# Level products of a gated recurrence in 32-column parts of TensorE, and pair products in its row halves

## The chip, the cores and the metric

The kernel runs on one core of one Trainium2 chip. The metric is the device time of one execution in microseconds (us). TensorE is called PE below, its weight loads PEld, VectorE DVE, ScalarE ACT, GpSimd POOL. A line number such as L1396 is the line of the kernel that issued an instruction.

## The reference, cut to what matters

One decoder layer: RMSNorm, one wide projection `w_in` of the normed rows (256 prompt tokens and 8 sequences of 8 sampled tokens, 320 rows in all), two recurrent branches, two projections merged by gates, an output projection and a final norm. Both recurrences are evaluated in blocks of tokens.

Branch A (16 heads of 64 channels, RWKV-7) is a delta rule with a matrix state:

```
s = s * w_t - (s kk_t)(kk_t * a_t)^T + v_t k_t^T ;  y_t = s r_t
```

Branch B (8 heads of 128 channels, HGRN2) is a gated linear recurrence:

```
b = cumsum(log_g);  o = (q * exp(b)) @ s
att[t, s] = sum_d q[t, d] k[s, d] exp(b[t, d] - b[s, d])   for s <= t, else 0
o += att @ v;       s = exp(b_last) * s + (k * exp(b_last - b))^T v
```

The change touches how `att` of branch B, and the matrix of all pairs of tokens in a block of 64 (`g2`) of branch A, are computed.

## The kernel before, in words

After a start stage that norms and transposes the inputs, one long stage computes the projection and both recurrences, head pair by head pair (`p` from 0 to 7: two heads of branch A, one of branch B). Its streams are the matmuls of the big projection (tile `mps`): weights are split into two float32r parts, `whi` and `wlo`, and each weight tile of 128x128 meets the 320 rows three times. All other matmuls of this stage (tiles `a`, `b`, `y`, called small products here) belong to the recurrences. They are plain float32, and each stands in the trace as two passes, two pairs of a weight load and a matmul.

The order of this stage is made by `Recorder`: every operation is recorded (so nearly all carry line L1396), `link` finds what depends on what, and `order` runs a list schedule over the engines with modelled costs. On PE a small product that is ready goes ahead of the streams. A product whose weights have at most 64 rows or columns uses a part of the array and has a `mode` other than (128, 128); such products wait until at least `APART` = 10 streams have run since the last of their kind, and those of `hgrn` until they have been ready for `WAIT` = 6000 ns (as the model sees it), so that several can share one change of the array's mode. After the eighth head pair the gate tiles of `NFILL` = 4 further column blocks (`sga`) are streams that the last head's recurrence can run beside. Then the merging stage begins (L338 to L340, with its own main tiles first, then `ppa` and `ppb`), and last the output stage (`po`).

In `rwkv`, `bk2` holds for each of four blocks of 64 prompt tokens (and a fifth block of 64 sampled tokens) the decayed keys, with two heads of 64 channels stacked on the partitions. `arp` holds the queries with zeros for the other head, so that one product of 128 rows gives both heads' pairs: five products of 128x128 weights with 256 columns, in three PSUM tiles `pg`. DVE multiplies them by the mask `mk` into `g2`.

In `hgrn`, `level(sz, tag)` makes the decayed keys and queries (`kq`) for pairs of neighbouring blocks of `sz` tokens with ACT (exponentials) and DVE (products), and moves the running decays `F` and `R` up one level. `products` multiplies 128 tokens by 128 tokens, twice (`j` = 0, 1), although only blocks on the diagonal are kept; `keep` copies those by the mask `mu8` into `att`, which POOL clears first for each head. The order is: products inside blocks of 8 (`k0`, `q0`) and of level 8; the states' products `pos` of the eight sampled sequences (`qz` by `s0`, 32 columns of weights each, in four column parts of the array); the work on the sampled states; levels 16, 32 and 64 with their products (`pl`); then the products with `vt`.

Of the kernel before, what the change touches and what calls it, by code (L numbers as in the profile page):

```python
# [9 lines left out]
F32 = mybir.dt.float32  # L10
# [7 lines left out]
NP_ = 256  # L18
# [29 lines left out]

class Op:
    __slots__ = ("eng", "fn", "args", "kw", "cost", "lat", "uses", "mode", "passes", "cols", "stream",  # L50
                 "succ", "npred", "ready", "rank", "block", "margin", "wait", "port", "hold", "dma", "n")


def span_of(ap):
# [14 lines left out]
class Recorder:  # L69
# [2 lines left out]

    def __init__(self, engines, is_big):
        self.real, self.ops, self.spans, self.is_big = engines, [], {}, is_big
        self.block, self.wait = None, 0

    def proxy(self, eng):
        rec, real = self, self.real[eng]
# [6 lines left out]
    def add(self, eng, name, fn, args, kw):  # L85
# [16 lines left out]
        o.lat = self.LAT[eng]  # L102
        o.dma = "dma" in name
        o.mode = None
        o.block = self.block
# [5 lines left out]
        if eng == "PE":  # L111
# [41 lines left out]

    def link(self):

        writers, readers = {}, {}
        for o in self.ops:
            o.succ, pred = [], {}
            for name, p0, p1, m, wr, psum in o.uses:
# [22 lines left out]
            o.npred = len(pred)  # L182
            for q, data in pred.values():
# [90 lines left out]
def hybrid_step(ctx, tc, x_prompt, x_sample, state_rwkv, state_hgrn, state_shift, norm_g, w_in,  # L274
# [19 lines left out]
    def ctile(shape, name, dt=F32, pool=rconst):  # L294
        return pool.tile(shape, dt, name=name, tag=name)
# [59 lines left out]
    with tc.tile_pool(name="start", bufs=1) as st, \  # L355
# [59 lines left out]
        def keep_ge(ap, pattern, base, cm, fill=0.0):  # L415
            G.affine_select(out=ap, in_=ap, pattern=pattern, compare_op=ALU.is_ge, fill=fill,
                            base=base, channel_multiplier=cm)
# [36 lines left out]
                         mk[:, 0, x].rearrange("p (s i) -> p s i", i=8), blk)  # L454


        mf = st.tile([64, 3, 64], F32, name="mf")
        mu8 = ctile([128, 3, 64], "mu8", U8)
        G.memset(mf, 1.0)
        for n, sz in enumerate((8, 8, 16)):  # L460
            if n == 0:
                mfh = mf[:, 0].rearrange("p (b i) -> p b i", i=8)
                keep_ge(mf[:, 0], [[1, 64]], 0, -1)
                keep_ge(mfh, [[-8, 8], [0, 8]], 0, 1)
                keep_ge(mfh, [[8, 8], [0, 8]], 7, -1)
                continue
            lv = mf[:, n].rearrange("p (b two s) -> p b two s", two=2, s=sz)
            nb = 32 // sz
# [216 lines left out]
    def ring(pool, tag, shape, bufs, dt, size, clear=False):  # L685
# [12 lines left out]
        if len(shape) == 2:  # L698
# [2 lines left out]
        return t_.rearrange(f"p ({' '.join(names)}) -> p {' '.join(names)}", **dict(zip(names, shape[1:])))  # L701

    SIZES = {"uK": 384, "uS": 384, "uE": 384, "uA": 320, "uB": 384, "uQ": 320, "big": 512, "s0t": 512, "v": 384,
             "w1": 384, "w2": 320, "w3": 320, "ks": 128, "ket": 256}


    CLEAR = {"uB", "uE", "ys", "rhs", "rhs2", "k3", "vm", "w1", "vt"}

    def at(name, shape=(128, NT), tag=None, bufs=1, dt=F32):
        tag = tag or name  # L710
# [48 lines left out]
    def rwkv(p, r, k, vp, za):  # L759
# [105 lines left out]

        g2 = at("g2", (128, 5, 2, 2, 64))
        M = at("M", (128, 3, 2, 64), tag="uE")
        for g in range(3):
            ps = aps("pg")
            n = 2 if g < 2 else 1  # L870
            for c_ in range(n):
                ci = 2 * g + c_
                T.matmul(ps[:, 256 * c_:256 * c_ + 256], bk2[:, ci].rearrange("p j t -> p (j t)"),
                         arp[:, ci].rearrange("p x h t -> p (x h t)"), start=True, stop=True)
            m = mk[:, 0:2] if g < 2 else mk[:, 2:3]
            V.tensor_mul(g2[:, 2 * g:2 * g + n].rearrange("p c x h t -> p (c x) h t"),
                         ps[:, :256 * n].rearrange("p (a h t) -> p a h t", h=2, t=64),
                         m.rearrange("p c x t -> p (c x) t")[:, :, None].to_broadcast([128, 2 * n, 2, 64]))


        half = lambda ps, n: ps[:, :192 * n].rearrange("p (a x t) -> p a x t", a=n, x=3)[:, :, 0:3:2]
# [243 lines left out]
    def hgrn(hd, q, k, v, zb):  # L1125
# [40 lines left out]
        V.tensor_mul(k0[:, :NT], k0[:, :NT], k)  # L1166

        att = bt("att", (128, 2 * 128 + 64))
        G.memset(att, 0.0)

        def level(sz, tag):
            half = lambda t_: t_[:, :NP_].rearrange("p (b two s) -> p b two s", two=2, s=sz)
            kq = bt("kq", (128, NP_), tag=tag)
            if sz in (32, 64):

                side = [kq[:, 128 * x:128 * x + 128].rearrange("p (b s) -> p b s", s=sz) for x in range(2)]
            else:
                side = [half(kq)[:, :, x] for x in range(2)]
            for x, e in enumerate((R, F)):
                S.activation(side[x], half(e)[:, :, x], AF.Exp)  # L1180
# [10 lines left out]
        def products(ps, o_, kq, q_):  # L1191
            for j in range(2):
                tk_ = slice(128 * j, 128 * j + 128)
                T.matmul(ps[:, o_ + 128 * j:o_ + 128 * j + 128], kq[:, tk_], q_[:, tk_], start=True, stop=True)

        def keep(ps, o_, n):
            own = lambda t_, c_: t_.rearrange("p (j c t) -> p j c t", c=2, t=64)[:, :, c_]
            for c_ in range(2):
                sl = HS[c_]
                V.copy_predicated(own(att[sl, :NP_], c_), mu8[sl, None, n].to_broadcast([64, 2, 64]),  # L1200
                                  own(ps[sl, o_:o_ + NP_], c_))
# [16 lines left out]
        V.tensor_mul(es[:, 1], es[:, 1], k[:, NP_:])  # L1218

        ps = bps("pos")  # L1220
        for si in range(NSEQ):
            j = si % 4
            T.matmul(ps[32 * j:32 * j + 32, 128 * (si // 4):128 * (si // 4) + 128], qz[:, si, :], s0[:, si, :],
                     start=True, stop=True)
# [37 lines left out]
        for j in range(2):  # L1262
            for b in range(2):
                o_ = 64 * j + 32 * b
                V.tensor_copy(att[64 * b:64 * b + 32, 128 * j + 64 * b + 32:128 * j + 64 * b + 64],
                              ps[o_:o_ + 32, 256 + o_:288 + o_])
            V.tensor_copy(att[0:64, 128 * j + 64:128 * j + 128], ps[HS[j], 384 + 64 * j:448 + 64 * j])

        kq128 = bt("kq", (128, 2, 128), tag="w3")
        ke = bt("ke", (128, 128), tag="w1")  # L1270
# [40 lines left out]
    def shift_state():  # L1311
        for g, (s_, n) in enumerate(((0, 5), (5, 4))):
# [265 lines left out]
```

## Time and profile before

| | before |
|---|---|
| median of 3 runs | 1157.26 us (1156.6 to 1157.67) |
| the profiled execution's own time | 1155.96 us |
| its span, first to last instruction | 1154.3 us |
| mean granted clock of PE | 0.998 |
| busy share of the span: PE, DVE, ACT, POOL | 98%, 67%, 58%, 18% |

A row of the trace that begins with two numbers gives start and length in us. A group gives a count, then the busy time and the mean length of one. PE's matmuls overlap: one that is listed with 0.31 us may be followed by the next after 0.15 us, so the distance between starts is what a matmul costs, not its length.

### The profile page before, as it was taken

To read this page: it belongs to the slowest core of one execution; us is meant where nothing else is said; L and a number is where in the kernel's file an instruction comes from. 1 tells how busy PE (TensorE), PEld (TensorE's weight loads), DVE (VectorE), ACT (ScalarE), POOL (GpSimd) and SP (SyncE) were. 2 spreads that over 40 slices of the span, in tenths; PEclk is the share of its full clock that TensorE was granted. 3 is DMA by queue.
4 is the path that set the end of the run, shared out by engine and by line. 5 is a ranking of instruction groups with operands and counts; after the bars stand their busy time and mean duration, and the time that the engine had idled before them with its cause. 6 is when DMAs were issued, how large, how long until landed. Compare 5 with 4: busy or idle time off the path is not lost.

```text
span 1154.3 us, 20774 instructions
## 1 busy us (share of the span) xinstructions
PE 1135.7 (98%) x7816; PEld 1097.9 (95%) x7816; DVE 775.9 (67%) x1634; ACT 669.2 (58%) x1483; POOL 208.0 (18%) x405
## 2 busy tenths in 40 slices
PE   6999999999999999999999999999999999999997
PEld 6999999999999999999999999999999999998886
DVE  8778878877887888878788686544444444436632
ACT  6766766667666667567667667444444444435322
POOL 9432223222311321421321310000000000000000
PEclk9999999999999999999999999999999999999999
DMA  6745435535445435436435434555555555577512
GB/s 180 199 117 127 129 102 136 142 92 132 129 113 146 117 93 150 131 81 169 120 93 162 115 105 132 148 152 153 152 147 148 151 154 151 146 253 254 182 41 91
DMA packets 283096, 159.69 MB, mean 138 GB/s; under 512 B 22893, under 2 KB 273264, under 8 KB 282356
## 3 DMA queue, kind: packets, MB, share of 16 engines
q1 hardware_dynamic: 282996, 158.37, 48.6%
q8 instruction: 61, 1.00, 0.4%
q14 instruction: 39, 0.32, 0.1%
HBM read 148.53 MB, written 9.81 MB: 137 GB/s over the span
## 4 chain that ended last, share of the span: by engine, by line
PE 96%; POOL 2%; DVE 1%; ACT 1%; issue 0%; DMA 0%; ACTq 0%; POOLq 0%
PE mps L1396 41%; PE a L1396 13%; PE mps L338 6%; PE mps L340 6%; PE mps L339 6%; PE b L1396 4%; PE po L1479 3%; PE po L1481 3%; PE po L1480 3%; PE ppb L338 2%; PE ppa L338 2%; PE ppb L340 2%; PE ppa L340 2%; PE ppa L339 2%; PE ppb L339 2%; PE po L1484 1%
## 5 line engine op out<-in xcount | busy, mean ns | idle before, releaser
L1396 PE MATMUL mps<-hhi,wlo 128*128 128x320 f32 x1088 | 344.9, 317 | 0.0
L1396 PE MATMUL mps<-hlo,whi 128*128 128x320 f32 x1088 | 344.7, 317 | 0.0
L1396 PE MATMUL mps<-hhi,whi 128*128 128x320 f32 x1088 | 344.6, 317 | 0.0
L1396 PEld LDWEIGHTS mps<-hlo,whi 128*128 128x128 f32 x1088 | 204.9, 188 | 3.3 <-issue 3.0
L1396 PEld LDWEIGHTS mps<-hhi,wlo 128*128 128x128 f32 x1088 | 205.0, 188 | 2.7 <-issue 2.4
L1396 PEld LDWEIGHTS mps<-hhi,whi 128*128 128x128 f32 x1088 | 205.0, 188 | 0.8 <-issue 0.4
L329 DVE TENSOR_TENSOR wlo<-raw,whi 128x1024 fp32r<-128x1024 f32 x88 | 107.8, 1225 | 125.0 <-ACT whi L328 124.8
L328 ACT CAST whi<-raw 128x1024 fp32r<-128x1024 f32 x88 | 92.3, 1048 | 163.3 <-PE mps L339 104.8
L1396 ACT CAST whi<-raw 128x1024 fp32r<-128x1024 f32 x134 | 140.6, 1049 | 77.2 <-PE mps L1396 75.8
L1396 DVE TENSOR_TENSOR wlo<-raw,whi 128x1024 fp32r<-128x1024 f32 x134 | 167.5, 1250 | 24.4 <-ACT whi L1396 23.1
L339 PE MATMUL mps<-hlo,whi 128*128 128x320 f32 x448 | 138.5, 309 | 0.0
L338 PE MATMUL mps<-hhi,whi 128*128 128x320 f32 x448 | 138.5, 309 | 0.0
L340 PE MATMUL mps<-hhi,wlo 128*128 128x320 f32 x448 | 138.5, 309 | 0.0
L340 PEld LDWEIGHTS mps<-hhi,wlo 128*128 128x128 f32 x448 | 84.1, 188 | 0.0
L338 PEld LDWEIGHTS mps<-hhi,whi 128*128 128x128 f32 x448 | 84.1, 188 | 0.0
L339 PEld LDWEIGHTS mps<-hlo,whi 128*128 128x128 f32 x448 | 84.1, 188 | 0.0
L1468 DVE TENSOR_TENSOR wlo<-raw,whi 128x1024 fp32r<-128x1024 f32 x32 | 38.5, 1222 | 39.1 <-ACT whi L1467 39.0
L1467 ACT CAST whi<-raw 128x1024 fp32r<-128x1024 f32 x32 | 33.1, 1051 | 48.4 <-DMA raw<-in_w_out_dram 22.4
L1479 PE MATMUL po<-whi,mhi 128*128 128x512 f32 x128 | 50.1, 391 | 0.7 <-DVE gbt L1436 0.7
L1481 PE MATMUL po<-wlo,mhi 128*128 128x512 f32 x128 | 50.0, 391 | 0.0
L1480 PE MATMUL po<-whi,mlo 128*128 128x512 f32 x128 | 50.0, 391 | 0.0
L339 PE MATMUL ppb<-ybl,whi 128*128 128x320 f32 x128 | 39.6, 309 | 0.0
(409 smaller groups left out, 2304.0 us busy)
## 6 DMA issues: line engine op xcount, KB each, us to landing
raw<-in_w_in_dram SPq DMA_DIRECT2D x194, 512.0 KB
raw<-in_w_out_dram SPq DMA_DIRECT2D x32, 512.0 KB
raw<-in_proj_a_dram SPq DMA_DIRECT2D x16, 512.0 KB
raw<-in_proj_b_dram SPq DMA_DIRECT2D x16, 512.0 KB
s<-in_state_hgrn_dram SPq DMA_DIRECT2D x8, 512.0 KB
out_dram<-s SPq DMA_DIRECT2D x8, 512.0 KB
s<-in_state_rwkv_dram SPq DMA_DIRECT2D x8, 256.0 KB
out_dram<-s SPq DMA_DIRECT2D x8, 256.0 KB
```

The costliest lines, as they stand in the source:

```text
L328: S.copy(hi[:, ks], raw[:, ks])
L329: sub.tensor_sub(lo[:, ks], raw[:, ks], hi[:, ks].bitcast(F32))
L338: T.matmul(dst, hi[:, q, :], xhi[:, k, :], start=(k == 0), stop=False)
L339: T.matmul(dst, hi[:, q, :], xlo[:, k, :], start=False, stop=False)
L340: T.matmul(dst, lo[:, q, :], xhi[:, k, :], start=False, stop=(k == nk - 1))
L1396: o.fn(*o.args, **o.kw)
L1467: S.copy(hi, raw)
L1468: V.tensor_sub(lo, raw, hi.bitcast(F32))
L1479: T.matmul(pt, h, hi, start=first, stop=False)
L1480: T.matmul(pt, l, hi, start=False, stop=False)
L1481: T.matmul(pt, h, lo, start=False, stop=end)
L1484: T.matmul(pt, h, hi, start=first, stop=False)
```

## The change

In `rwkv` the pair products of the four prompt blocks become eight: for each head 64 rows (`HS[h]`) of `bk2` and `arp`, 128 columns of weights and 128 columns that stream, the two heads alternating in the upper and lower row half of the array, each head in a PSUM tile of its own. The fifth product stays. DVE's masking multiplications stay three, with other views.

In `hgrn` all four levels are made at once, before the states' products. Every level product is now made by 32 tokens: 32 columns of weights and 32 that stream (64 at the last level), in the column part where those 32 tokens lie, so that the result holds only tokens of one block of 32. There are 34 of them, recorded right behind the eight states' products in one group: 24 for the first three levels, 4 for level 32, 4 for level 64, 2 for the sampled tokens. They replace nine products of full weight tiles. Masks shrink to 32x32; three masked copies of DVE go to a new tile `attc`, four copies of ACT move its blocks to `att`, two masked copies take the sampled tokens, and the six copies of levels 32 and 64 stay. `att` and `attc` are cleared once. `kq16`, `kq32` and `kq64` use other buffers.

`Recorder` gets groups: the members of one share their dependencies and the highest rank of them, so that they stand together on PE, and a cost that counts all parts of the array as running at once.

```diff
@@ Recorder.add
-            o.cost = o.passes * max(load, stream / min(2, 128 // o.mode[1]))
+            side = 128 // o.mode[1] * (128 // o.mode[0] if o.group else 1)
+            o.cost = o.passes * max(max(load, stream) / side, 7) if o.group else o.passes * max(load, stream / min(2, side))
@@ Recorder.link
+        for members in groups.values():
+            own = {o.n for o in members}
+            shared = {}
+            for o in members:
+                for n, (q, data) in preds[o.n].items():
+                    if n not in own:
+                        shared[n] = q, data or shared.get(n, (q, False))[1]
+            for o in members:
+                preds[o.n].update(shared)
...
+        for members in groups.values():
+            top = max(o.rank for o in members)
+            for o in members:
+                o.rank = top
@@ start stage
-        mf = st.tile([64, 3, 64], F32, name="mf")
-        mu8 = ctile([128, 3, 64], "mu8", U8)
+        mf = st.tile([32, 3, 32], F32, name="mf")
+        mu8 = ctile([128, 3, 32], "mu8", U8)
...
-        for sl in HS:
-            G.tensor_copy(mu8[sl], mf)
+        for g in range(4):
+            G.tensor_copy(mu8[32 * g:32 * g + 32], mf)
@@ rwkv
-        for g in range(3):
-            ps = aps("pg")
-            n = 2 if g < 2 else 1
-            for c_ in range(n):
-                ci = 2 * g + c_
-                T.matmul(ps[:, 256 * c_:256 * c_ + 256], bk2[:, ci].rearrange("p j t -> p (j t)"),
-                         arp[:, ci].rearrange("p x h t -> p (x h t)"), start=True, stop=True)
...
+        banks = [aps("pg") for _ in HS]
+        side_by_side([((banks[h][:, 128 * ci:128 * ci + 128], bk2[HS[h], ci].rearrange("p j t -> p (j t)"),
+                        arp[HS[h], ci, :, h]), dict(start=True, stop=True)) for ci in range(4) for h in range(2)])
+        for h in range(2):
+            V.tensor_mul(g2[:, 0:4, :, h].rearrange("p (a c) x t -> p a (c x) t", c=2),
+                         banks[h].rearrange("p (a c t) -> p a c t", a=2, t=64),
+                         mk[:, 0:2].rearrange("p c x t -> p (c x) t")[:, None].to_broadcast([128, 2, 4, 64]))
+        ps = aps("pg")
+        T.matmul(ps[:, :256], bk2[:, 4].rearrange("p j t -> p (j t)"), arp[:, 4].rearrange("p x h t -> p (x h t)"),
+                 start=True, stop=True)
@@ hgrn
         att = bt("att", (128, 2 * 128 + 64))
-        G.memset(att, 0.0)
...
-        kq8 = level(8, "w2")
-        ps = bps("pg")
-        products(ps, 0, k0, q0)
-        products(ps, 256, kq8, kq8)
-        keep(ps, 0, 0)
-        keep(ps, 256, 1)
+        kq8, kq16, kq32, kq64 = level(8, "w2"), level(16, "o"), level(32, "ket"), level(64, ("s1", "ks"))
...
+        work = [((ps[32 * j:32 * j + 32, 128 * g:128 * g + 128], qz[:, 4 * g + j], s0[:, 4 * g + j]))
+                for g in range(2) for j in range(4)]
+        tile32 = lambda g, c0, a_, b_: work.append((pg[32 * g:32 * g + 32, c0:c0 + b_.shape[-1]], a_, b_))
+        for n, (a_, b_) in enumerate(((k0, q0), (kq8, kq8), (kq16, kq16))):
+            for j in range(2):
+                for g in range(4):
+                    tk_ = slice(128 * j + 32 * g, 128 * j + 32 * g + 32)
+                    tile32(g, 64 * n + 32 * j, a_[:, tk_], b_[:, tk_])
+        for g in range(4):
+            tile32(g, 192, kq32[0][:, 32 * g:32 * g + 32], kq32[1][:, 32 * g:32 * g + 32])
+        for g in range(4):
+            tile32(g, 224, kq64[0][:, 32 * g:32 * g + 32], kq64[1][:, 64 * (g // 2):64 * (g // 2) + 64])
+        for g in range(2):
+            tk_ = slice(NP_ + 32 * g, NP_ + 32 * g + 32)
+            tile32(g, 288, k0[:, tk_], q0[:, tk_])
+        side_by_side([(x_, dict(start=True, stop=True)) for x_ in work])
+        attc = bt("attc", (128, 2, 32))
+        for n in range(3):
+            V.copy_predicated(attc, mu8[:, None, n].to_broadcast([128, 2, 32]),
+                              pg[:, 64 * n:64 * n + 64].rearrange("p (j t) -> p j t", t=32))
+        for g in range(4):
+            own = slice(32 * g, 32 * g + 32)
+            S.copy(att[own, :NP_].rearrange("p (j t) -> p j t", j=2)[:, :, own], attc[own])
+            if g < 2:
+                V.copy_predicated(att[own, NP_ + 32 * g:NP_ + 32 * g + 32], mu8[own, 0], pg[own, 288:320])
...
-        T.matmul(ps[:, 128:192], k0[:, NP_:], q0[:, NP_:], start=True, stop=True)
-        V.copy_predicated(att[0:64, NP_:], mu8[0:64, 0], ps[0:64, 128:192])
...
-        kq16, kq32, kq64 = level(16, "w3"), level(32, "w2"), level(64, "w1")
-        ps = bps("pl")
-        products(ps, 0, kq16, kq16)
-        T.matmul(ps[:, 256:384], kq32[:, 0:128], kq32[:, 128:256], start=True, stop=True)
-        T.matmul(ps[:, 384:512], kq64[:, 0:128], kq64[:, 128:256], start=True, stop=True)
-        keep(ps, 0, 2)
@@ new
+    def side_by_side(products):
+        book.group = len(book.ops)
+        for args, kw in products:
+            T.matmul(*args, **kw)
+        book.group = None
```

## Rows read from the trace of the kernel before

**Rows 1.** The page: span, busy time of each engine, chain by engine.
```profile
span 1154.3 us, 20774 instructions
PE 1135.7 (98%) x7816; PEld 1097.9 (95%) x7816; DVE 775.9 (67%) x1634; ACT 669.2 (58%) x1483; POOL 208.0 (18%) x405
PE 96%; POOL 2%; DVE 1%; ACT 1%; issue 0%; DMA 0%; ACTq 0%; POOLq 0%
```
**Rows 2.** Busy time by engine, recurrence stage: length, PE, PEld, DVE, ACT, POOL, granted clock.
```profile
30.00:700.00 670.00, 668.98 (x4905) 653.58 (x4904) 543.60 (x1333) 451.39 (x1146) 179.83 (x349) 1.00 0.46 126
```
**Rows 3.** PE's waits: total us, times, longest.
```profile
PE mps L591 <- POOL wlo L598: 0.6, 1, 0.6
```
**Rows 4.** Timeline of PE around one head pair's pair products (`arp`, `bk`).
```profile
62.69 0.31 PE L1396 MATMUL mps<-hhi,wlo 128*128 128x320 f32 x1
62.84 2.32 PE L1396 MATMUL a<-arp,bk 128*128 128x256 f32 x10
64.81 0.50 PE L1396 MATMUL mps<-hhi,whi 128*128 128x320 f32 x1
65.14 0.31 PE L1396 MATMUL mps<-hlo,whi 128*128 128x320 f32 x1
```
**Rows 5.** Instructions on tiles `w`: durations min/median/max, first and last start, forms.
```profile
L1396 PE MATMUL b<-w x96: 270/275/377, 91.2 to 681.2; 128*128 128x128 f32 x96
L1396 PE MATMUL b<-w,w x48: 217/275/275, 90.1 to 669.7; 128*128 128x128 f32 x32, 128*128 128x64 f32 x16
```
**Rows 6.** Timeline of PE at two runs of level products, a stream between.
```profile
666.58 0.61 PE L1396 MATMUL b<-w,w 128*128 128x128 f32 x4
666.94 0.39 PE L1396 MATMUL mps<-hhi,wlo 128*128 128x320 f32 x1
667.17 0.60 PE L1396 MATMUL b<-w 128*128 128x128 f32 x4
```
**Rows 7.** Timeline of PE around the states' products of the last head.
```profile
676.05 0.31 PE L1396 MATMUL mps<-hhi,whi 128*128 128x320 f32 x1
676.29 0.64 PE L1396 MATMUL b<-s,qz 128*32 128x128 f32 x16
676.86 0.41 PE L1396 MATMUL mps<-hlo,whi 128*128 128x320 f32 x1
677.11 0.27 PE L1396 MATMUL a<-ident,sr 128*128 128x128 f32 x1
```
**Rows 8.** The first head's states' products, matmuls begun by 100.772 and by 101.3.
```profile
100.75 0.32 PE L1396 MATMUL b<-s,qz 128*32 128x128 f32 x4
...
100.75 0.64 PE L1396 MATMUL b<-s,qz 128*32 128x128 f32 x16
```
**Rows 9.** Their weight loads begun by 100.88, when four matmuls had begun.
```profile
100.75 0.16 PEld L1396 LDWEIGHTS b<-s,qz 128*32 128x32 f32 x8 [0.19 <-issue]
```
**Rows 10.** Instructions on tile `att`.
```profile
L1396 DVE COPY_PREDICATED att<-mu,b x56: 214/296/313, 92.0 to 683.2; 64x128 f32<-64x128 uint8 x48, 64x64 f32<-64x64 uint8 x8
L1396 POOL MEMSET att<- x8: 358/364/373, 39.5 to 619.8; 128x320 f32 x8
```
**Rows 11.** Groups by shape: the nearest ACT copy, and POOL's mask work.
```profile
L1396 ACT COPY uE<-uB 64x64 f32<-64x64 f32 x16 | 3.9, 245 | 0.2
...
L473 POOL CAST mu<-mf 64x192 uint8<-64x192 f32 x2 | 2.2, 1098 | 0.1
...
L416 POOL TENSOR_SCALAR_AFFINE_SELECT mf<-mf 64x64 f32<-64x64 f32 x3 | 1.2, 416 | 0.0
```
**Rows 12.** Instructions on tile `arp`: the pair products of all heads.
```profile
L1396 PE MATMUL a<-arp,bk x80: 377/379/380, 62.8 to 640.7; 128*128 128x256 f32 x80
```
**Rows 13.** The chain that ended last, at the end of the recurrence stage.
```profile
706.98 0.15 PE a L1396
707.12 11.29 PE mps L1396 x77
```

More of the change, by code (lines that the diff above doesn't have):

```diff
@@ L50 @@
     __slots__ = ("eng", "fn", "args", "kw", "cost", "lat", "uses", "mode", "passes", "cols", "stream",
-                 "succ", "npred", "ready", "rank", "block", "margin", "wait", "port", "hold", "dma", "n")
+                 "succ", "npred", "ready", "rank", "block", "margin", "wait", "port", "hold", "dma", "n", "group")
 def span_of(ap):
@@ L74, in __init__ @@
         self.real, self.ops, self.spans, self.is_big = engines, [], {}, is_big
-        self.block, self.wait = None, 0
+        self.block, self.wait, self.group = None, 0, None
     def proxy(self, eng):
@@ L104, in add @@
         o.mode = None
-        o.block = self.block
+        o.block, o.group = self.block, self.group
         o.margin, o.wait = 0, self.wait
@@ L154, in link @@
     def link(self):
-        writers, readers = {}, {}
+        writers, readers, preds = {}, {}, {}
         for o in self.ops:
             o.succ, pred = [], {}
+            preds[o.n] = pred
             for name, p0, p1, m, wr, psum in o.uses:
@@ L181, in link @@
             pred.pop(o.n, None)
-            o.npred = len(pred)
-            for q, data in pred.values():
+        groups = {}
+        for o in self.ops:
+            if o.group is not None:
+                groups.setdefault(o.group, []).append(o)
+        for members in groups.values():
[7 more added lines that the diff above has]
+                preds[o.n].update(shared)
+        for o in self.ops:
+            o.npred = len(preds[o.n])
+            for q, data in preds[o.n].values():
                 q.succ.append((o, data))
@@ L462, in hybrid_step @@
                 mfh = mf[:, 0].rearrange("p (b i) -> p b i", i=8)
-                keep_ge(mf[:, 0], [[1, 64]], 0, -1)
-                keep_ge(mfh, [[-8, 8], [0, 8]], 0, 1)
-                keep_ge(mfh, [[8, 8], [0, 8]], 7, -1)
+                keep_ge(mf[:, 0], [[1, 32]], 0, -1)
+                keep_ge(mfh, [[-8, 4], [0, 8]], 0, 1)
+                keep_ge(mfh, [[8, 4], [0, 8]], 7, -1)
                 continue
             lv = mf[:, n].rearrange("p (b two s) -> p b two s", two=2, s=sz)
-            nb = 32 // sz
+            nb = 16 // sz
             G.memset(lv[:, :, 0, :], 0.0)
@@ L703, in hybrid_step @@
     SIZES = {"uK": 384, "uS": 384, "uE": 384, "uA": 320, "uB": 384, "uQ": 320, "big": 512, "s0t": 512, "v": 384,
-             "w1": 384, "w2": 320, "w3": 320, "ks": 128, "ket": 256}
-    CLEAR = {"uB", "uE", "ys", "rhs", "rhs2", "k3", "vm", "w1", "vt"}
+             "w1": 384, "w2": 320, "w3": 320, "ks": 128, "ket": 256, "o": NT}
+    CLEAR = {"uB", "uE", "ys", "rhs", "rhs2", "k3", "vm", "w1", "vt", "att", "attc"}
     def at(name, shape=(128, NT), tag=None, bufs=1, dt=F32):
@@ L867, in rwkv @@
         M = at("M", (128, 3, 2, 64), tag="uE")
-        for g in range(3):
-            ps = aps("pg")
-            n = 2 if g < 2 else 1
-            for c_ in range(n):
-                ci = 2 * g + c_
-                T.matmul(ps[:, 256 * c_:256 * c_ + 256], bk2[:, ci].rearrange("p j t -> p (j t)"),
-                         arp[:, ci].rearrange("p x h t -> p (x h t)"), start=True, stop=True)
[L875 to L878, printed above, removed]
+        banks = [aps("pg") for _ in HS]
[8 more added lines that the diff above has]
+                 start=True, stop=True)
+        V.tensor_mul(g2[:, 4], ps[:, :256].rearrange("p (x h t) -> p x h t", x=2, h=2),
+                     mk[:, 2, :, None].to_broadcast([128, 2, 2, 64]))
         half = lambda ps, n: ps[:, :192 * n].rearrange("p (a x t) -> p a x t", a=n, x=3)[:, :, 0:3:2]
@@ L1168, in hgrn @@
         att = bt("att", (128, 2 * 128 + 64))
-        G.memset(att, 0.0)
         def level(sz, tag):
             half = lambda t_: t_[:, :NP_].rearrange("p (b two s) -> p b two s", two=2, s=sz)
-            kq = bt("kq", (128, NP_), tag=tag)
             if sz in (32, 64):
-                side = [kq[:, 128 * x:128 * x + 128].rearrange("p (b s) -> p b s", s=sz) for x in range(2)]
+                half_ = bt("kq", (128, NP_), tag=tag) if sz == 32 else None
+                kq = [half_[:, 128 * x:128 * x + 128] for x in range(2)] if sz == 32 else \
+                    [bt("kq", (128, 128), tag=t_) for t_ in tag]
+                side = [x.rearrange("p (b s) -> p b s", s=sz) for x in kq]
             else:
+                kq = bt("kq", (128, NP_), tag=tag)
                 side = [half(kq)[:, :, x] for x in range(2)]
@@ L1188, in level @@
             return kq
[L1191 to L1201, printed above, removed]
-        kq8 = level(8, "w2")
-        ps = bps("pg")
-        products(ps, 0, k0, q0)
-        products(ps, 256, kq8, kq8)
-        keep(ps, 0, 0)
-        keep(ps, 256, 1)
+        kq8, kq16, kq32, kq64 = level(8, "w2"), level(16, "o"), level(32, "ket"), level(64, ("s1", "ks"))
         es = bt("es", (128, 2, 64))
@@ L1220, in hgrn @@
         ps = bps("pos")
[L1221 to L1224, printed above, removed]
+        pg = bps("pg")
+        work = [((ps[32 * j:32 * j + 32, 128 * g:128 * g + 128], qz[:, 4 * g + j], s0[:, 4 * g + j]))
[23 more added lines that the diff above has]
+                V.copy_predicated(att[own, NP_ + 32 * g:NP_ + 32 * g + 32], mu8[own, 0], pg[own, 288:320])
+        for j in range(2):
+            for b in range(2):
+                V.tensor_copy(att[64 * b:64 * b + 32, 128 * j + 64 * b + 32:128 * j + 64 * b + 64],
+                              pg[64 * j + 32 * b:64 * j + 32 * b + 32, 192:224])
+            V.tensor_copy(att[0:64, 128 * j + 64:128 * j + 128], pg[HS[j], 224:288])
         sot = bt("sot", (128, 256), tag="ket")
@@ L1253, in hgrn @@
         Y.dma_start(s_hgrn[0, :, hd].rearrange("s k v -> k s v"), s0)
-        kq16, kq32, kq64 = level(16, "w3"), level(32, "w2"), level(64, "w1")
-        ps = bps("pl")
-        products(ps, 0, kq16, kq16)
-        T.matmul(ps[:, 256:384], kq32[:, 0:128], kq32[:, 128:256], start=True, stop=True)
-        T.matmul(ps[:, 384:512], kq64[:, 0:128], kq64[:, 128:256], start=True, stop=True)
-        keep(ps, 0, 2)
[L1262 to L1267, printed above, removed]
         kq128 = bt("kq", (128, 2, 128), tag="w3")
```

## The prediction

> **What bounds the kernel now.** Read the page's busy times and its chain by engine first [rows 1]: PE is busy for 98% of the span and the chain that ended last is 96% PE. Next the table by stretches [rows 2]: in the 670 us that hold the recurrences PE is busy for 669, at a granted clock of 1.00 (the 2.4 GHz level), DVE for 544 and ACT for 451. Last PE's waits: of those that the change can touch the longest is one of 0.6 us in the start stage [rows 3]. So in the recurrence stage time is what PE's instructions cost at their starts; what an engine beside it gains or loses is worth nothing until it comes near 669. The streams and the merging and output stages are the same before and after. The sum is therefore PE time alone, head pair by head pair, eight times.
>
> **Level products removed.** By the code nine products of full 128-column weights leave each head: two of `k0` by `q0`, two each of levels 8 and 16, one each of levels 32 and 64, and one for the sampled tokens, which streams only 64 columns. With two passes each that is 18 passes, and the trace has them: 96 and 48 over eight heads [rows 5]. A run of four passes starts at 666.58, one stream follows, the next run starts at 667.17 [rows 6]. Less a stream's own distance of 0.147 (77 streams in 11.29 us [rows 13]) that leaves 0.44 us, 0.11 a pass. The short product costs nearly the same, since its weights are as wide. A few runs come a little cheaper when they stand against other small products, so I take 1.95 us for the 18 and not 1.98.
>
> **Level products added.** 34 products of two passes are 68 passes, in a mode of the array that the states' products use already. These are the nearest rows. Four passes had begun by 100.772, within 0.022 us, so starts in different column parts can follow each other by about 7 ns [rows 8]. Their lengths as a run grow from 0.32 for four to 0.64 for sixteen: three more sets of four in 0.32 us, 0.107 a set, which is what one pass of 128 columns costs on the whole array [rows 6, 8]. So four parts stream at once. With 32 columns in place of 128 a set streams for a quarter of that, 0.027 us, and four starts at 7 ns take as long. 28 products of 32 columns make 14 sets, 0.38 us; four of 64 columns two sets of 0.054, 0.11; the two of the sampled tokens half-filled sets, 0.05. Sum 0.54 us, 8 ns a pass. That is the low end. From above, the whole run of sixteen took 0.43 us without its mode changes, 27 ns a pass; if that pace is one of issue and not of columns, 68 passes cost 1.84 us. I take 0.54, because the seven-nanosecond starts are the only ones in the trace that wait for nothing else; 1.84 stays as a rival.
>
> A rule speaks against it. The 18 weight loads of a head become 68, and these must be hidden too. By 100.88 eight loads had begun while only four matmuls had [rows 8, 9]: the second set's weights go in while the first set streams, and sets follow at 0.107 with no room for a load between them. The Trainium skill, page "TensorE: Matmul & The Clock Gate", section "What overlaps and what doesn't", says that a weight load overlaps running matmuls only where the row group differs, and column parts all share their rows. By the rows the loads are hidden and the price is 0.54; by the rule each set would pay its load as well as its stream. The trace disagrees with that rule here, at 128 columns.
>
> **Mode changes.** The states' products had theirs before: between 676.05 and 677.11 lie that run and two streams, 1.06 us, less two streams 0.77, less the run's 0.43 leaves 0.33 for going in and out [rows 7]. The group keeps them: nothing is added. For the pair products they are new.
>
> **Pair products.** Before, ten passes of 256 columns: 62.84 to 65.14 holds them and one stream, 2.30 less 0.15, 2.15 us, 0.215 a pass [rows 4]. After: the fifth product keeps two such passes, 0.43. Eight products on half the rows are 16 passes of 128 columns; no row of this trace has two row halves in use at once. If they run side by side as the column parts do [rows 8], two at a time cost 0.11, together 0.88. If they run one after the other they cost 16 times 0.11, 1.76. With 0.33 for the mode the new price is 1.64 or 2.52. I take 1.64: weights and streams come from different partitions and the results go to two PSUM tiles, while the column parts already share more than that. Gain 0.51 us a head, or a loss of 0.37.
>
> **Other engines.** DVE loses six masked copies of 64x128 and one of 64x64 a head (about 2.0 us at 0.296 and 0.214) and gets three of 64 elements and two of 32 (about 1.1 us) [rows 10]. ACT gets four copies of 64 elements on 32 partitions, at most 0.245 each, 1 us a head [rows 11]; POOL loses a memset of 0.364 [rows 10]. The two PSUM buffers of branch B are now held together, which lengthens the head's own chain. All of this costs nothing while the streams cover it. The cover: a head pair takes (640.7 - 62.8) / 7, 82.5 us at the most, since the first start of a pass and the last of another are compared [rows 12]; DVE needs 544 / 670 of that, 67 us, and PE would need 80. At the end 77 streams, 11.29 us, run behind the last small product [rows 13], so a chain that ends up to 11 us later still stalls nobody; beyond that each us would count. Sampled states are now updated behind all levels, whose twelve ACT and twelve DVE operations are the same ones, only earlier.
>
> **Start stage.** POOL's mask selections of 64 columns (three of 0.416) become half as wide, its casts become four of half the size instead of two of 1.098 [rows 11]: between no change and 0.6 us less, the wait that PE has there [rows 3]. I take 0.3.
>
> **Sum.** Each head pair: -1.95 + 0.54 - 0.51 = -1.92 us; eight of them -15.4, with the start -15.7. On the profiled execution, 1155.96 us for a span of 1154.3, that is 1140.3; the median of the runs shown lies 1.3 above it, at 1157.26, which gives 1141.6.
>
> **Rivals.**
> *Row halves take turns.* The pair products then cost 0.37 more, not 0.51 less: -1.95 + 0.54 + 0.37 = -1.04 a head, -8.6 in all, 1148.7. For it: no row shows two row halves. Against it: the column parts.
> *Loads of narrow weights are not hidden.* A set then costs 0.054: 1.08 for the group, -1.38 a head, -11.3, 1145.9. For it: with 32 columns there is only 0.027 us to hide a load in. Against it: [rows 9]. The skill's rule above is this case.
> *A narrow pass has a floor.* At the run's mean of 27 ns a pass the 68 cost 1.84: -0.62 a head, -5.3, 1152.0. For it: no row shows starts that go on at 7 ns past a set of four. Against it: the run's pace equals that of full-width columns exactly, so columns explain it. The Trainium skill, page "TensorEngine Tiling (Array Packing)", section "Instruction Overhead", states such a floor: about 60 cycles a matmul whatever it streams, and the advice not to tile a dimension that is already small. At 2.4 GHz this is an estimate of 25 ns a pass, close to this case.
> *The other side: PE's instruction supply.* A head's group is 84 passes and as many loads back to back; the longest such run of before is 16 [rows 8]. If instructions queue ahead for a short run only, the rest come at the supply's own pace. All other terms save 1.95 + 0.51 = 2.46 us a head, so from 36 ns a pass on, the kernel is slower. At twice the mean of rows 8, 54 ns, the 68 cost 3.67: +1.21 a head, +9.4, 1166.7. Against it: sixteen came at 27 with no sign of a tail.
> *No change.* Two of the milder rivals together, or a chain that outgrows its cover by some 13 us.
>
> **How the numbers follow.** Chances: forecast 0.54 (its own range 1139 to 1145, to 12 ns a pass), row halves in turn 0.13, floor 0.12, loads 0.06, more gained than this 0.03 (runs that were interrupted less often; down to 1137), supply 0.08, no change 0.04. The range of 1137 to 1152.5 leaves out the last two, 0.12, and part of the floor case. A change of 0.2%, 2.3 us, is about what this measurement can tell from none: faster 0.88, the same 0.04, slower 0.08.
>
> **What would show it.** In the changed profile: the group should last about 1.0 us from its first to its last start, with starts 7 ns apart throughout; the pair products about 0.9 us for sixteen passes, in couples; the stretch of the recurrences shorter by about 15 us with PE as full as now; the merging stage unchanged. Wrong would be: starts in the group that spread to 27 ns or more, pair passes 0.11 apart singly, or waits of PE on `att`, `kq` or `g2`.

## The result and the profile after

The changed kernel takes 1142.42 us (four runs, 1142.3 to 1142.66) against 1157.47 for the kernel before (four runs, 1156.6 to 1158.74): a ratio of 0.9869, interval 0.9852 to 0.9886. 1141.6 was forecast. Of the runs below, one execution of the kernel with level products by column parts took 3950 us with PE slow throughout, and it is left out of the times.

The page of the changed kernel, its span, busy times and chain, against [rows 1]:

```profile
span 1141.0 us, 21733 instructions
PE 1124.7 (99%) x8280; PEld 1088.2 (95%) x8280; DVE 770.6 (68%) x1618; ACT 675.6 (59%) x1515; POOL 207.6 (18%) x401
PE 98%; POOL 1%; DVE 1%; ACT 0%; issue 0%; ACTq 0%; DVEq 0%; POOLq 0%
```

The second line of the three tells the kind of change: PE has 464 passes more (8 times 68 - 18 + 16 - 8) and 11 us less busy time. PE is as full as before. The recurrence stage by engine, against [rows 2], and PE's waits that the change could touch, against [rows 3]:

```profile
30.00:687.00 657.00, 656.56 (x5378) 641.81 (x5377) 536.73 (x1318) 457.69 (x1177) 180.35 (x343) 1.00 0.47 128
```
```profile
PE a L1425 <- POOL yz L1425: 0.3, 1, 0.3
PE mps L612 <- ACT hhi L529: 0.3, 1, 0.3
```

The pair products of the first head pair, in the timeline of PE (start, length), against [rows 4]; the second and third lines are the same stretch cut off at 63.26 and at 63.46, so that their counts tell how many passes had begun:

```profile
63.00 0.31 PE L1425 MATMUL mps<-hhi,wlo 128*128 128x320 f32 x1
63.24 0.38 PE L1425 MATMUL a<-arp,bk 64*128 64x128 f32 x2
63.24 0.49 PE L1425 MATMUL a<-arp,bk 64*128 64x128 f32 x4
...
63.24 1.16 PE L1425 MATMUL a<-arp,bk 64*128 64x128 f32 x16
64.33 0.41 PE L1425 MATMUL mps<-hhi,whi 128*128 128x320 f32 x1
64.58 0.31 PE L1425 MATMUL mps<-hlo,whi 128*128 128x320 f32 x1
64.73 0.60 PE L1425 MATMUL a<-arp,bk 128*128 128x256 f32 x2
64.97 0.50 PE L1425 MATMUL mps<-hhi,wlo 128*128 128x320 f32 x1
65.31 0.31 PE L1425 MATMUL mps<-hhi,whi 128*128 128x320 f32 x1
```

Passes begin two at a time; a run of two ends 0.11 us before a run of four. Sixteen passes and the way in and out of the mode take 1.09 us from start to next start. The group of level products of that head, against [rows 7, 8]; the three lines ahead of the second "..." are cut off at 104.13, 104.16 and 104.19:

```profile
103.64 0.65 PE L1425 MATMUL b<-s,qz 128*32 128x128 f32 x16
...
104.10 0.21 PE L1425 MATMUL b<-w,w 128*32 128x32 f32 x4
104.10 0.24 PE L1425 MATMUL b<-w,w 128*32 128x32 f32 x8
104.10 0.28 PE L1425 MATMUL b<-w,w 128*32 128x32 f32 x12
...
104.23 0.34 PE L1425 MATMUL b<-w 128*32 128x32 f32 x15
104.38 0.21 PE L1425 MATMUL b<-o 128*32 128x32 f32 x1
104.39 0.20 PE L1425 MATMUL b<-w 128*32 128x32 f32 x1
104.39 0.34 PE L1425 MATMUL b<-o 128*32 128x32 f32 x13
...
104.74 0.24 PE L1425 MATMUL b<-w,w 128*32 128x32 f32 x4
104.91 0.64 PE L1425 MATMUL a<-big,uv 128*64 128x512 f32 x1
```

The level products begin in sets of four, a set each 0.03 us: 16 passes from 104.10 to 104.23. From about 104.30 on, behind 25 of the 68, they spread: the last pass starts at 104.78. That is 68 passes in 0.68 us, 10 ns each on average and 11 in the second part. Last, the end of the stage in the chain, against [rows 13]:

```profile
694.62 0.14 PE a L1425
694.76 10.41 PE mps L1425 x71
```

71 streams still run behind the last small product, so the cover at the end has shrunk by less than 1 us.

Where PE's stage went, worked out from the starts (each instruction counts until the next one starts), in us. The first two columns leave a part of a small product's cost with the streams: the stream at 64.97 starts 0.03 us behind a pass of `arp`, and the next stream follows it only after 0.34. In the last two columns what a stream takes beyond its 0.147 is counted to the small products beside it (0.09 to a change of mode that follows, the rest to what stands ahead), so these are estimates.

```
                         by own starts      with the streams held up
                         before    after    before    after
streams (3264)           506.9     505.4    477.9     478.2
pair products             15.75     10.7     17.3      13.6
levels and states         17.6      10.1     20.4      10.9
all other small ones     148.9     148.6    173.6     172.2
stage                    689.1     674.9    689.1     674.9
```

By the last two columns the pair products give 3.7 us and the levels 9.5. The other 1.1 of the stage's 14.3 lie in products and streams that the change leaves as they are.

### The profile page after: what moved, and what is told of

Same layout as the page of the kernel before. It is cut to its first block, busy times and chain, and to the rows that moved or that the text cites. A ratio compares the mean times of both kernels' runs of the same rounds, so it can differ in the third digit from the quotient of the medians.

```text
span 1141.0 us, 21733 instructions
## 1 busy us (share of the span) xinstructions
PE 1124.7 (99%) x8280; PEld 1088.2 (95%) x8280; DVE 770.6 (68%) x1618; ACT 675.6 (59%) x1515; POOL 207.6 (18%) x401
## 4 chain that ended last, share of the span: by engine, by line
PE 98%; POOL 1%; DVE 1%; ACT 0%; issue 0%; ACTq 0%; DVEq 0%; POOLq 0%
PE mps L1425 42%; PE a L1425 12%; PE mps L359 6%; PE mps L361 6%; PE mps L360 6%; PE b L1425 3%; PE po L1508 3%; PE po L1510 3%; PE po L1509 3%; PE ppb L359 2%; PE ppa L359 2%; PE ppb L361 2%; PE ppa L361 2%; PE ppa L360 2%; PE ppb L360 2%; PE po L1514 1%
## 5 line engine op out<-in xcount | busy, mean ns | idle before, releaser
L359 PE MATMUL ppa<-yah,whi 128*128 128x320 f32 x128 | 39.6, 309 | 0.0
```

Of the source, the lines that this page charges most:

```text
L359: T.matmul(dst, hi[:, q, :], xhi[:, k, :], start=(k == 0), stop=False)
```

## The experiments

All are the changed kernel with one edit, but for the second, which is the kernel before with one part of the change, and the last but one, which has two edits. Medians stand beside 1142.4 us for the changed kernel and 1157.4 to 1157.5 for the kernel before, which was timed again beside each of them.

**One part alone.** Levels only: the block of pair products put back.

```diff
-        banks = [aps("pg") for _ in HS]
-        side_by_side([... for ci in range(4) for h in range(2)])
+        for g in range(3):
+            ps = aps("pg")
...
```

> The changed kernel with branch A's pair products as they were before (ten passes of 256 columns, whole array). Theory (time is the sum of PE's starts, head by head): it loses the pair products' share. By the forecast's term 0.51 us a head, 1142.4 + 4.1 = 1146.5; by the rows of the changed kernel, where 16 passes in row halves and the two whole ones cost 10.7 us over eight heads against 15.8 before, 1147.5. Rival (the gain is the levels' alone and the row halves only shift work that was covered): 1142.4 to 1143.

Measured 1147.13 (1147.07 to 1147.44): the levels alone bring 10.3 us, and the pair products 4.7 beside them. Of the 4.7 the pair section itself, with the streams that it holds up, is 3.5 (17.1 to 13.6 in the two traces). Another 1.5 lie in the other small products, where PE waits 1.3 us in this version and 0.3 in the changed kernel; the levels give 0.2 the other way.

Pairs only (the edits of `rwkv` and the groups of `Recorder`, in the kernel before):

> The kernel before with branch A's pair products in row halves alone; branch B and its masks as before. Theory: 1157.4 less 4.1 (forecast) to 5.1 (rows of the changed kernel), 1152.3 to 1153.3, and with the levels alone it adds up to the whole change. Rival (row halves take turns, the couples of starts in the trace hide a lower rate): 1157 to 1160.

Measured 1154.34 (nine runs, 1153.67 to 1154.82), ratio 0.9974 (0.9964 to 0.9984): 3.05 us, less than either figure. The pair section itself costs the same 10.7 us in this trace as in the changed kernel's, or 13.7 with the streams that it holds up, 3.5 less than before. But the other small products cost 175.3 us here, 1.7 more than before, and PE waits in two places of the stage that the changed kernel's order does not have:

```profile
PE a L1426 <- DVE uv L1426: 1.0, 1, 1.0
PE a L1426 <- DVE ast L1426: 0.8, 1, 0.8
```

So the parts add to 13.3 of 15.05 us. Their own sections do add up: 9.7 for the levels alone and 9.5 in the whole change, 3.5 and 3.7 for the pairs. The rest lies in what the list schedule makes of the other small products in each version; the last runs take that up.

**Order of the pair products.**

```diff
-                        arp[HS[h], ci, :, h]), dict(start=True, stop=True)) for ci in range(4) for h in range(2)])
+                        arp[HS[h], ci, :, h]), dict(start=True, stop=True)) for h in range(2) for ci in range(4)])
```

> The changed kernel with the eight pair products issued head after head: four of the upper row half, then four of the lower, instead of alternating. Theory (PE starts matmuls in the order of the program, so that two halves run together only when neighbours in the program use different halves): 16 passes at 0.11 one after the other, 0.88 us more a head, 1149.4. Rival (each half works through its own products whatever the order): 1142.4.

Measured 1146.42 (1146.31 to 1146.63), 4.0 us more, between the two. The timeline of PE, cut off at 63.20, 63.51, 63.96 and past the end:

```profile
62.97 0.49 PE L1425 MATMUL a<-arp,bk 64*128 64x128 f32 x2
62.97 0.71 PE L1425 MATMUL a<-arp,bk 64*128 64x128 f32 x4
62.97 1.26 PE L1425 MATMUL a<-arp,bk 64*128 64x128 f32 x12
62.97 1.71 PE L1425 MATMUL a<-arp,bk 64*128 64x128 f32 x16
```

Four passes come singly, eight of both halves within 0.45 us, four singly again. The whole is 1.71 us long instead of 1.16: 0.55 us a head, 4.4 in all. By the raw starts (each instruction's own start in the trace) the first pass of the lower half begins 5 ns behind the fifth of the upper half's eight, so it goes ahead of three that stand before it in the program. From there each half goes on by itself. Neither expectation had this: PE keeps to the program's order only beyond a few passes. The next run shows the same more plainly.

**Order of the level products.** All of part 0 first, then part 1, and so on:

```diff
...
+        work[8:] = [x_ for g in range(4) for x_, g_ in zip(work[8:], col_part) if g_ == g]
         side_by_side([(x_, dict(start=True, stop=True)) for x_ in work])
```

> The changed kernel with the 34 level products issued column part by column part (all of part 0, then all of part 1, ...) instead of part after part in turn. Theory (order of the program): at most neighbours at the borders overlap, 60 passes at 27 ns and 8 at 54 instead of 0.68 us for all, 1.4 us more a head, 1153.5. Rival (each part works through its own): 1142.4, with starts as regular as before.

Measured 1151.45 to 1153.64 in three runs. The starts are read from one more run of the same kernel:

> The same kernel as in the run by column parts, for a look at the starts. Theory (order of the program): within a head's group the 68 level passes take about 2.0 us instead of 0.68, with starts 27 ns apart and seldom two at once.

Measured 1151.91, 9.5 us more. PE's timeline where the third column part ends and the fourth begins:

```profile
186.38 0.29 PE L1430 MATMUL b<-w 128*32 128x32 f32 x4
186.51 0.29 PE L1430 MATMUL b<-o 128*32 128x32 f32 x4
186.64 0.20 PE L1430 MATMUL b<-ket 128*32 128x32 f32 x1
186.64 0.22 PE L1430 MATMUL b<-w,w 128*32 128x32 f32 x1
186.67 0.20 PE L1430 MATMUL b<-ket 128*32 128x32 f32 x1
186.69 0.20 PE L1430 MATMUL b<-w,w 128*32 128x32 f32 x1
186.70 0.22 PE L1430 MATMUL b<-ks,s 128*32 128x64 f32 x1
```

Eight passes of one part take 0.26 us, 0.032 each, and by their starts the 68 take 1.85 us. The two passes of a product stay neighbours: the tiles follow one another unmixed within a part. At the border the third part still has `ket` and `ks,s` to do, two passes each, and in the program the fourth part's first `w,w` stands behind them. Its first pass starts 6 ns behind the first of `ket`, ahead of the other three. In all eight heads it is so, and in the run before it was three passes as well. Sets of four starts in the changed kernel fit the same account: a pass whose part is busy can be overtaken by one that stands up to three places behind it. The figure of three comes from these traces alone; no run varied it. So parts run side by side only where the program alternates them within a few passes.

**What spreads the starts.** The level list issued twice:

```diff
+        work += work[8:]
         side_by_side([(x_, dict(start=True, stop=True)) for x_ in work])
```

> The changed kernel with the list of 34 level products issued twice in the group, writing the same results again: 68 passes more a head. In the changed kernel's group the first 40 passes start in sets of four at 7 ns, then the starts spread to 11 ns on average. Theory (after some 40 passes PE is held by the supply of its instructions): the added passes all come at 11 ns, 0.77 us a head, 1148.6, and no set of four at 7 ns appears in the second list. Rival (columns alone set the price, the spread belongs to these products): the second list starts as the first one did, 0.53 us, 1146.7.

Measured 1151.77 (1151.09 to 1152.62), 9.35 us more, above both. The second list has no set of four at 7 ns. Its 68 passes take 0.64 us a head, 9.4 ns each, 5.1 us in all. The other 4 us are three waits that only this kernel has, as PE's waits show in sum and the timeline for one of them:

```profile
PE b L1426 <- issue: 4.0, 3, 2.4
```
```profile
264.18 0.28 PE L1426 MATMUL b<-ks,s 128*32 128x64 f32 x5
265.20 0.24 PE L1426 MATMUL b<-ks,s 128*32 128x64 f32 x1 [0.74 <-issue]
```

"issue" is a wait for nothing that the profile shows. This one stands in the middle of products whose inputs are long there, so that PE having no next instruction is what is left; that is argued, not shown. The two others stand shortly behind a group, at the transpose of `es`, and what they wait for is open.

The same number of instructions with more columns:

```diff
-                    tile32(g, 64 * n + 32 * j, a_[:, tk_], b_[:, tk_])
+                    work.append((pg[32 * g:32 * g + 32, 128 * n + 64 * j:128 * n + 64 * j + 64], a_[:, tk_],
+                                 b_[:, None, tk_].to_broadcast([128, 2, 32])))
...
```

> The changed kernel in which the 24 products of the first three levels stream their 32 columns twice, 64 columns a pass, with the same number of instructions; the second copy is not read. Theory (supply): a set of four passes now takes 54 ns by its columns, 13 ns a pass, more than the 11 of the supply, so the spread of the starts goes away there and 48 passes take 0.65 us instead of about 0.48: 0.17 us a head, 1143.8. Rival (the spread is a cost of the products themselves, in columns or weight loads): all of it doubles, 0.48 us a head, 1146.2.

Measured 1143.35 (1143.3 to 1143.79), 0.9 us more. The timeline shows even sets throughout, no mixing of tiles at the borders:

```profile
103.73 0.41 PE L1426 MATMUL b<-w,w 128*32 128x64 f32 x16
103.95 0.41 PE L1426 MATMUL b<-w 128*32 128x64 f32 x16
104.18 0.41 PE L1426 MATMUL b<-o 128*32 128x64 f32 x16
104.40 0.24 PE L1426 MATMUL b<-ket 128*32 128x32 f32 x8
```

16 passes each 0.22 us, 14 ns a pass, up to the end of the three levels. Twice the columns cost a fifth of a microsecond a head: where the starts spread, columns are not what is paid. What is paid goes by passes. Each pass brings a weight load as well as a matmul, and these runs do not tell the two apart.

The states' products last:

```diff
+        work = work[8:] + work[:8]
         side_by_side([(x_, dict(start=True, stop=True)) for x_ in work])
```

> The changed kernel with the states' eight products behind the 34 level products in the group instead of ahead of them. Theory (supply, instructions queue ahead while PE streams or while the states' products take 27 ns a pass): the time stays at 1142.4; the level passes again start at 7 to 8 ns for some 24 and then spread. Rival (the spread begins at a fixed count of about 40 passes from the start of the group): the first 40 level passes come in sets of four at 7 ns.

Measured 1142.43 in one run, the time that the theory gave, but the trace gives neither count:

```profile
103.34 0.33 PE L1426 MATMUL b<-w,w 128*32 128x32 f32 x16
103.49 0.31 PE L1426 MATMUL b<-w 128*32 128x32 f32 x16
103.62 0.36 PE L1426 MATMUL b<-o 128*32 128x32 f32 x15
103.79 0.21 PE L1426 MATMUL b<-ket 128*32 128x32 f32 x1
```

Now the 32 passes of `w` come at 8 to 9 ns, and the spread begins with `o`: by the raw starts 33 passes come in sets of four, where the theory had some 24 and the rival 40. In the changed kernel it was 41 passes, 16 of them the states' and 25 of the levels. So the quick start is not a fixed count of passes from the start of the group, and the states' slower pace does not leave it untouched either. What sets the count is open.

**The cover.** The three masked copies and ACT's four done four times each:

```diff
-        for n in range(3):
+        for n in (0, 1, 2) * 4:
             V.copy_predicated(attc, ...
...
-            S.copy(att[own, :NP_]...
+            for _ in range(4):
+                S.copy(att[own, :NP_]...
```

> The changed kernel with the three masked copies into attc and the four copies of ACT into att each done four times: about 2 us more of DVE and 2.4 us more of ACT a head, on the way from the group to the products with vt. Theory (everything but PE is covered by the streams): no change, 1142.4 within 0.5. Rival (the chain of a head, longer since the change, is close to its cover): part of 8 times 4.4 us shows, 1145 or more, with waits of PE on att.

Measured 1143.29 (1143.25 to 1143.39), 0.9 us more, for 2.1 us of DVE and 2.9 of ACT a head, 40 us in all. PE has no wait on `att`, and 79 streams still run behind the last small product. The cover holds; the 0.9 is more than the 0.5 allowed, and the next runs show that another order of the same work moves the time by more than that.

**A version that goes on, and the order's own share.** The fifth pair product in row halves too:

```diff
-        banks = [aps("pg") for _ in HS]
+        banks = [aps("pg") for _ in range(3)] + [ring(psy, "y", [128, 512], 1, F32, None)]
+        dst = lambda h, ci: banks[h][:, 128 * ci:128 * ci + 128] if ci < 4 else banks[2 + h][:, :128]
...
-                        ... for ci in range(4) for h in range(2)])
+                      for ci in range(5) for h in range(2)])
...
```

> The changed kernel with the fifth pair product (sampled tokens) in row halves too, two products of 64 rows and 128 columns in the same group, the lower half's in the PSUM bank of the y tiles: two couples of passes at 0.11 instead of two whole passes at 0.215 in a place of their own. DVE masks it in two operations instead of one. Theory (PE's starts): 0.21 to 0.3 us a head less, 1140.0 to 1140.7. Rival (the fourth PSUM tile, which the group must now wait for, and the longer group delay the head): 1142.4 or more.

Measured 1143.46 (1143.45 to 1144.41): 1.0 more, not 2 less. The pair section, counted with the streams that it holds up, is shorter by 1.5 us (13.6 to 12.1), a little less than the least expected, 1.7. But PE waits 2.5 us in the stage, most of it in three places:

```profile
PE a L1424 <- DVE st L1424: 0.9, 1, 0.9
PE a L1424 <- DVE pp L1424: 0.8, 1, 0.8
...
PE a L1424 <- DVE ast L1424: 0.6, 1, 0.6
```

The same kernel, and as a control the changed kernel itself, with a larger margin in the list schedule:

```diff
-    APART, MARGIN, WAIT, OVER = 10, 250, 6000, 130
+    APART, MARGIN, WAIT, OVER = 10, 500, 6000, 130
```

> The kernel with all five pair products in row halves, and the margin that the list schedule adds before a small product doubled (250 to 500 ns), so that PE meets fewer products whose inputs are late. In the run without it the pair section is 0.21 us a head shorter, as worked out, but PE waits 2 us more in the stage. Theory (the gain was lost to waits that the order happens to have): waits fall, 1140.5 to 1142. Rival (the group with the fourth PSUM tile delays the head whatever the order): 1143.5.

> The changed kernel itself with the doubled margin, the control to the other: it tells what another order of the same work is worth. Theory: PE's waits are only 0.4 us of its stage, so 1142 to 1143. Rival: the changed kernel's order leaves as much as the others' do, 1141 or less.

Measured 1140.41 (1139.94 to 1141.57) for five products in halves, ratio to before 0.9853 (0.9837 to 0.987), and 1140.88 (1140.67 to 1142.3) for the control, 0.9859 (0.9845 to 0.9874). The first one's waits in the stage fall from 2.5 to 0.3 us. But the control gains 1.5 us from the same edit, as its rival had it (one of its four runs, at 1142.3, does not), and its other small products cost 2.0 us less in the trace. Its waits in the stage, 0.2 us, are about the changed kernel's 0.3, so the gain lies in how the small products stand among the streams. If the control's 1.5 us holds for any version, half of the 3.05 us between the two versions with five products in halves is the order's. Between the two versions stand 0.5 us, inside both ranges, so what the fifth product is worth in time stays open between nothing and the 1.7 us worked out, which is what its section gives in the two traces (13.8 to 12.1). Both are faster than the changed kernel by 1.5 to 2 us, 0.1 to 0.2%.

## Why the prediction was right, point by point

*What bounds the kernel.* Right: PE is full before and after, the streams cost the same, and what follows the recurrence stage takes 436.0 us in both traces.

*Level products removed and added.* -1.41 us a head were forecast, 11.3 in all; levels alone measured 10.3 by the medians. Their own section gives 9.5, 1.19 a head: the removed passes were worth 1.88 where 1.95 was taken, and the added ones cost 0.69 where 0.54 was. The second is the term that was most mis-sized. From first to last start the 68 passes took 0.68 us. The first 25 of them came near the price that was read off the states' products, 0.031 us a set where 0.027 was taken. The rest were held by something that goes by passes and not by columns, which is the rival on the other side in a mild form (10 ns a pass on average, against the 36 from which the kernel loses). The forecast had starts 7 ns apart throughout and a group of about 1.0 us from first to last start. The first failed and the group takes 1.14; the time came out because the spread is small.

*Loads of weights.* Hidden, as the rows had it. A set of four passes with 32 columns of weights and 32 of stream follows the last one after 0.03 us, where load and stream in turn would take the 0.054 of the rival. (The rival's 1.08 us doubles the streams of 64 columns with the rest; one load of 0.027 a set gives 1.03, and 1145.5 for 1145.9.) The rule of the Trainium skill, page "TensorE: Matmul & The Clock Gate", section "What overlaps and what doesn't", that a load overlaps only across row groups, does not hold for column parts in this trace. The same section of the Trainium skill also says that matmuls start strictly in the order of the program. These traces agree beyond a few passes (1.85 us instead of 0.68 for the levels by part), but not within them: there a pass starts ahead of three that stand before it.

*A floor for narrow passes.* Not there across parts: starts lie 7 ns apart in a set. Within one part 32 columns cost 0.031 us, so nothing can be said of a floor below that.

*Pair products.* Row halves run side by side, couples at 0.11 us, 0.51 us a head forecast. Beside the levels the measured share is 4.7 us, alone 3.05; 4.1 was forecast. The section itself, with its streams, gives 3.5 to 3.7 in every trace, 0.46 a head at most; the dearer mode of the next point accounts for what is missing. The rival of halves in turn is out by the trace.

*Mode changes.* From 63.00 to 64.58 in the changed kernel lie two streams and 16 passes in couples: 1.58 less 0.29 less 0.88 is 0.41 for going in and out, where 0.33 was taken.

*Other engines.* DVE lost 5.3 us in all where 7 were worked out, ACT gained 6.4 where at most 8 were; nothing of it shows. Copies done four times cost 0.9 us of the 40 that they add, and whether that is the cover or another order is not shown. (640.7 - 62.8) / 7 is 82.6, not 82.5.

*Start stage.* Wrong by a little: 0.3 us of gain was taken; in this profile the stage's first stream begins at 30.1 instead of 29.1. The control with the same start code, in the trace of tile `mps`:

```profile
L1425 PE MATMUL mps<-hhi,whi x66: 305/309/397, 29.3 to 59.9; 128*128 128x320 f32 x66
```

begins at 29.3, so the 0.8 between them belongs to the execution and not to the change. PE's wait for POOL there, which was to shrink, is gone from the changed kernel's profile, but the control still has it:

```profile
PE mps L612 <- POOL wlo L619: 0.7, 1, 0.7
```

*The sum.* -15.7 was forecast; the medians give -15.05, the profiled executions -13.3. The kernel before was profiled in an execution 1.5 us below its median of four, which is the larger part of that difference. And the agreement to 0.8 us is partly luck. The two sections that the sum prices gave 13.2 us of the 15.4 forecast for them. The other small products, for which the sum has no term, gave 1.4 more in the stage. The order that the list schedule makes is what moves those: the control's margin moved the time of the same work by 1.5 us.

## What to carry to other kernels

Where small products use a part of TensorE's array, price them by the set of parts that run at once and let the program alternate the parts, product by product; the same products in another order cost nearly three times as much here. Around 10 ns a pass the number of passes is the price and not the columns: twice the columns in 48 passes cost 0.2 us more of 0.68. A wider and shorter list of products should then be worth a try; no run here shortened one. When a hand-made scheduler orders the work, run the old and new version under a second setting of it before trusting differences of a few tenths of a per cent.

## What the runs showed of the hardware

Four float32 passes of 32 columns in the four column parts start within 0.02 us, and the next four follow after 0.031. Two passes of 128 columns in the two row halves start 6 to 7 ns apart, and the next two follow after 0.11. Going into the row halves and out again cost 0.41 us.

A burst of narrow passes (a weight load each) begins quickly, for 41 passes where the first 16 were slow ones and for 33 where none was, and goes on at 9 to 11 ns a pass. With 152 passes in a burst PE once stood still in the middle of it, 0.96 us from one start to the next, which 84 passes never did.

Starts are not strictly in the order of the program. A pass whose part of the array is free started ahead of up to three passes of a busy part: at every border between column parts, and at the border of the row halves. That is why eight products ordered half by half ran partly side by side, 1.71 us between 1.16 for alternating halves and the 2.0 that sixteen single passes would take.
